# Residual, flushes and norm sums of a Strassen down projection, in a decoder layer on one core

## The chip, the cores and the metric

The kernel runs on one core of a Trainium2 chip. The metric is device time in microseconds of one execution. Before the change three timed runs took 2051.57, 2054.89 and 2056.43 us; the median is 2054.89 us.

## The reference, cut to what matters

One decoder layer for 1024 prompt rows and 32 sample rows that share all weights, in fp32. The two feed-forward blocks hold most of the work:

```python
x = x + 0.5 * _swiglu(_rms(x, g1), w1g, w1u, w1d)   # D = 1024, D_FF = 2816
z = _rms(x, gm) @ w_in                               # attention and short convolution
...
x = x + concat([attn_out, conv_out]) @ w_out
x = x + 0.5 * _swiglu(_rms(x, g2), w2g, w2u, w2d)
x = x + sigmoid(_rms(x, gp) @ w_ple_gate) * (p @ w_ple_proj)

def _swiglu(h, w_gate, w_up, w_down):
    return (jax.nn.silu(h @ w_gate) * (h @ w_up)) @ w_down
```

Each block is a gate-up projection (into 2816 columns) and a down projection (back into 1024), and each is followed by an RMS norm that the next projection needs.

## The kernel before, in words

**Layout.** All activations are kept transposed: `X[m]`, m = 0 to 7, is 128 of the 1024 features by all 1056 rows. The rows are worked in two chunks of 528 (`HC`), each in halves of 264 (`HH`). A matmul is 128x128 weights against 128x264, and each product is made of three matmuls, since weights and activations are split into a high and a low part (lines 799 to 801 in the down projection, 440 to 442 in gate-up).

**Seven products for eight.** Gate-up and down use a Strassen-Winograd scheme: seven block products, numbered 1 to 7, serve a 2x2 block of outputs. `segment` (464) issues them in the order 1, 5, 7 of the quad before, 2, 6, 3 and 4 of the quad before. After each product, `step` evacuates PSUM, casts that product's weights for the quad to come (`follow`; ACT casts in line 360, DVE takes the rest in 361), runs what hangs on the step (`then`), and takes two entries off the list `hops`.

**Pairs.** The 22 blocks of hidden features are joined into 11 pairs. `hop_steps` (485) makes from a pair's two blocks the seven operands of the scheme (sums on POOL, splits on ACT and DVE) and stores them to DRAM (`hop`, SP's queue, lines 512 and 516). The down projection reads them back through POOL's queue (842), 528 KB each, seven a pair; SBUF holds four pairs at a time.

**The down projection** walks the list `FLUSH` of 17 entries (row, first pair, end): output rows `row` and `row + 4` over those pairs, 44 pair-rows in all. For each entry SP loads four weight slabs (766) into six buffers, and POOL makes four sums of them (770 to 773). `put` (803) adds a finished PSUM half into X on DVE (806); `load_x` (844) has put the residual, the layer's input, into X first, eight loads of 528 KB at the start of the stage through SP's queue. The last pair, 10, is made while entries 1 and 2 run, through borrowed places (`FRAG10`), and the load of pair 3 stands behind it.

**The end of the stage.** `last_row` tells after which entry a row is complete. `norm_hook` (986) then squares the rows (ACT 281, added up on POOL 282) and splits them for the next projection (`prep`, ACT 293 and DVE 294). `norm_r` (301) sums over the partitions by matmul, does a chain of small DVE instructions for the inverse root, and spreads the result by matmul (318), as one step. The first weight unit of the next projection (`wget`, 512 KB, cast in 179 and 180) is loaded when that projection asks for it.

**What sets the order.** The code's order is a priority only: the program is built with `schedule_with_timeline_sim=True` (1605), so each engine's queue is laid out from a simulated timeline, and an instruction whose inputs are there in that simulation may come long before its place in the code. On the chip each queue then runs in that fixed order.

## Time and profile before

| | |
|---|---|
| median of 3 runs | 2054.89 us (2051.57 to 2056.43) |
| the profiled execution | 2056.14 us, its span 2054.4 us |
| TensorE busy / mean granted clock | 1961.2 us (95%) / 0.973 |
| DVE, ACT, POOL busy | 1388.2, 750.4, 864.2 us |
| DMA moved | 311 MB |
| down projections, from the first matmul of line 799 to the last of line 801 | 517 to 794 us and 1686 to 1955 us |

The profiled execution takes 1.7 us more than its span, which runs from the first to the last instruction. A granted clock of 1.00 is the 2.4 GHz level and 0.50 the 1.2 GHz level; a figure between is the mean of both over a stretch. "Idle before" is time in which an engine had no work in hand, with what ended it.

### The profile page before, as it was taken

The numbers are of one execution on the slowest core, as the hardware profiler recorded it, in microseconds if no ns is written. First come the engines' busy times: TensorE is split into PE (matmuls) and PEld (weight loads), VectorE is DVE, ScalarE is ACT, GpSimd is POOL, SyncE is SP. The second block draws the span as 40 slices with busy tenths as digits, with TensorE's granted clock in tenths as the row PEclk, the third lists the DMA queues.
The fourth block names the chain that finished last, engine by engine and source line by source line (L and its number), as shares of the span: only waits on it lengthen the run. The fifth ranks groups of instructions, "written<-read, shape, count | busy, mean of one in ns | idle before, by whom it ended". The sixth has DMA issues, their size and how long they took to land.

```text
span 2054.4 us, 38467 instructions
## 1 busy us (share of the span) xinstructions
PE 1961.2 (95%) x14639; PEld 1906.3 (93%) x14639; DVE 1388.2 (68%) x2635; ACT 750.4 (37%) x1590; POOL 864.2 (42%) x880
## 2 busy tenths in 40 slices
PE   7999999999699998999999899999999987999999
PEld 6999999999699997999887799999999987999898
DVE  7748877776666676456585367687777756666864
ACT  5324444444222243314344233344444432222531
POOL 2436665555444444003221124375555464443410
PEclk8999999999899998999999899999999998999999
DMA  7126754445976725101012331465454488775231
GB/s 254 67 79 204 229 168 133 153 157 175 359 236 222 246 93 175 36 20 42 21 34 82 100 110 48 140 221 166 143 166 132 133 280 302 247 233 187 80 136 50
DMA packets 184941, 311.15 MB, mean 151 GB/s; under 512 B 20289, under 2 KB 121033, under 8 KB 184628
## 3 DMA queue, kind: packets, MB, share of 16 engines
q1 hardware_dynamic: 160244, 220.23, 33.0%
q0 software_dynamic: 23648, 87.28, 12.4%
q8 instruction: 116, 1.90, 0.4%
q10 hardware_dynamic: 864, 1.18, 0.2%
q14 instruction: 69, 0.57, 0.1%
HBM read 202.50 MB, written 107.82 MB: 151 GB/s over the span
## 4 chain that ended last, share of the span: by engine, by line
PE 83%; DVE 6%; DMA 6%; issue 2%; ACT 1%; POOL 1%; SPq 0%; DVEq 0%; ACTq 0%; POOLq 0%
PE ps L440 11%; PE ps L441 11%; PE ps L442 11%; PE ps L799 7%; PE ps L801 6%; PE ps L800 6%; PE ps L332 4%; PE ps L334 4%; PE ps L333 4%; PE ps L1352 2%; PE ps L1351 2%; PE ps L1350 2%; PE ps L594 2%; PE ps L593 2%; PE ps L592 2%
## 5 line engine op out<-in xcount | busy, mean ns | idle before, releaser
L440 PE MATMUL ps<-bh_a,wh_a 128*128 128x264 f32 x2128 | 604.7, 286 | 16.6 <-DMA x_a<-in_xT_dram 6.7
L441 PE MATMUL ps<-bh_a,wl_a 128*128 128x264 f32 x2128 | 605.3, 285 | 0.0
L442 PE MATMUL ps<-bl_a,wh_a 128*128 128x264 f32 x2128 | 600.5, 284 | 0.0
L440 PEld LDWEIGHTS ps<-bh_a,wh_a 128*128 128x128 f32 x2128 | 400.3, 189 | 20.6 <-issue 12.7
L441 PEld LDWEIGHTS ps<-bh_a,wl_a 128*128 128x128 f32 x2128 | 401.4, 189 | 0.0
L442 PEld LDWEIGHTS ps<-bl_a,wh_a 128*128 128x128 f32 x2128 | 401.1, 189 | 0.0
L799 PE MATMUL ps<-pair_a,vh_a 128*128 128x264 f32 x1232 | 355.0, 293 | 34.7 <-ACT vh_a L360 17.5
L800 PE MATMUL ps<-pair_a,vl_a 128*128 128x264 f32 x1232 | 353.8, 288 | 0.3 <-DVE vl_a L361 0.2
L801 PE MATMUL ps<-pair_a,vh_a 128*128 128x264 f32 x1232 | 353.2, 289 | 0.0
L806 DVE SCALAR_TENSOR_TENSOR x_a<-ps,x_a 128x264 f32<-128x264 f32 x476 | 198.4, 427 | 133.8 <-PE ps L801 116.2
L799 PEld LDWEIGHTS ps<-pair_a,vh_a 128*128 128x128 f32 x1232 | 235.4, 193 | 41.2 <-ACT vh_a L360 19.4
L800 PEld LDWEIGHTS ps<-pair_a,vl_a 128*128 128x128 f32 x1232 | 237.3, 193 | 0.8 <-DVE vl_a L361 0.8
L801 PEld LDWEIGHTS ps<-pair_a,vh_a 128*128 128x128 f32 x1232 | 236.4, 192 | 0.0
L332 PE MATMUL ps<-xnh_a,whi_a 128*128 128x384 f32 (+1 forms) x528 | 173.3, 329 | 12.5 <-DVE x_a L1442 6.5
L333 PE MATMUL ps<-xnh_a,wlo_a 128*128 128x384 f32 (+1 forms) x528 | 171.8, 326 | 0.4 <-DVE wlo_a L180 0.4
L334 PE MATMUL ps<-xnl_a,whi_a 128*128 128x384 f32 (+1 forms) x528 | 171.8, 326 | 0.0
L361 DVE TENSOR_TENSOR wl_a<-ws_a,wh_a 128x512 fp32r<-128x512 f32 x152 | 132.6, 872 | 36.3 <-ACT wh_a L360 36.2
L385 POOL TENSOR_TENSOR ws_a<-wr_a,wr_a 128x512 f32<-128x512 f32 x38 | 50.9, 1339 | 211.5 <-DMA wr_a<-in_w2gu_dram 87.1
L360 ACT CAST vh_a<-dws_a 128x384 fp32r<-128x384 f32 (+2 forms) x136 | 62.9, 467 | 201.1 <-PE ps L801 180.7
L842 POOL DMA_DIRECT2D pair_a<-hop x154 | 83.7, 545 | 116.6 <-PE ps L801 69.8
L360 ACT CAST wh_a<-ws_a 128x512 fp32r<-128x512 f32 x152 | 94.4, 621 | 101.3 <-PE ps L442 87.5
L361 DVE TENSOR_TENSOR wl_a<-wr_a,wh_a 128x512 fp32r<-128x512 f32 x114 | 108.7, 955 | 12.7 <-ACT wh_a L360 11.6
(258 smaller groups left out, 4092.7 us busy)
## 6 DMA issues: line engine op xcount, KB each, us to landing
pair_a<-hop POOLq DMA_DIRECT2D x154, 528.0 KB, 6.8
hop<-sg_a SPq DMA_DIRECT2D x264, 264.0 KB
wr_a<-in_w1gu_dram SPq DMA_DIRECT2D x88, 256.0 KB
wr_a<-in_w2gu_dram SPq DMA_DIRECT2D x88, 256.0 KB
hop<-sge_a SPq DMA_DIRECT2D x88, 132.0 KB
dr_a<-in_w1d_dram SPq DMA_DIRECT2D x48, 192.0 KB
wraw_a<-in_win_dram SPq DMA_DIRECT2D x18, 512.0 KB
dr_a<-in_w2d_dram SPq DMA_DIRECT2D x48, 192.0 KB
```

The costliest lines, as they stand in the source:

```text
L332: nc.tensor.matmul(ps[:, :W], lhsT=wh, rhs=xh, start=(k == 0), stop=False)
L333: nc.tensor.matmul(ps[:, :W], lhsT=wl, rhs=xh, start=False, stop=False)
L334: nc.tensor.matmul(ps[:, :W], lhsT=wh, rhs=xl, start=False, stop=(k == n - 1))
L360: nc.scalar.copy(out=hi, in_=src)
L361: nc.vector.tensor_tensor(out=lo, in0=src, in1=hi.bitcast(F32), op=ALU.subtract)
L440: nc.tensor.matmul(ps[:, :HH], lhsT=wh[:, ks], rhs=bh, start=(start and k == 0), stop=False, skip_group_check=True)
L441: nc.tensor.matmul(ps[:, :HH], lhsT=wl[:, ks], rhs=bh, start=False, stop=False, skip_group_check=True)
L442: nc.tensor.matmul(ps[:, :HH], lhsT=wh[:, ks], rhs=bl, start=False, stop=last, skip_group_check=True)
L799: nc.tensor.matmul(ps[:, :HH], lhsT=wh[:, ks], rhs=bh, start=(start and i == 0), stop=False, skip_group_check=True)
L800: nc.tensor.matmul(ps[:, :HH], lhsT=wl[:, ks], rhs=bh, start=False, stop=False, skip_group_check=True)
L801: nc.tensor.matmul(ps[:, :HH], lhsT=wh[:, ks], rhs=bl, start=False, stop=(i == n - 1), skip_group_check=True)
L806: nc.vector.scalar_tensor_tensor(out=x, in0=ps[:, :HH], scalar=(0.25, -0.25)[up], in1=x, op0=ALU.mult, op1=ALU.add)
```

## The change

Seven things change, in both down projections. The residual is no longer loaded at the start: the first flush of each row writes its first PSUM part into X by ACT with a scale, and the residual comes later, in eight groups of two 264 KB loads, each added by POOL. The list of flushes is divided differently (still 17 entries and 44 pair-rows; the last entry has two pairs instead of one). The last pair is made at entries 5 and 6 from a copy in DRAM, where gate-up now stores blocks 20 and 21, and the load of pair 3 moves from entry 2 to entry 0. A down step takes one entry off `hops` instead of two. Splits of chunk 0 are all prepared with the row, those of chunk 1 all at the end, at other places. The next projection's first weight unit is loaded and split during the last entry. The norm's sums and its spreading stand apart, each behind a projection.

```diff
 FLUSH = [
-    (0, 0, 1), (1, 0, 2), (2, 0, 3), (3, 0, 3), (0, 1, 4), (1, 2, 5), (2, 3, 6), (3, 3, 6), (0, 4, 7),
-    (1, 5, 8), (2, 6, 9), (3, 6, 9), (0, 7, 10), (1, 8, 11), (2, 9, 11), (3, 9, 11), (0, 10, 11),
+    (0, 0, 1), (1, 0, 2), (2, 0, 2), (3, 0, 3), (0, 1, 4), (1, 2, 5), (2, 2, 5), (3, 3, 6), (0, 4, 7),
+    (1, 5, 8), (2, 5, 8), (3, 6, 9), (0, 7, 9), (1, 8, 11), (2, 8, 11), (3, 9, 11), (0, 9, 11),
 ]
+RES = {4: (2, 0), 7: (1, 0), 8: (2, 1), 9: (3, 0), 10: (0, 0), 11: (1, 1), 12: (3, 1), 13: (0, 1)}
...
-    def norm_r(c, name, s, d=2):
+    def norm_r(c, name, s):
...
-        after(d, stat)
+        return sums, spread
...
+    def hop_last(pr, c, src):
+        cell = {}
+        e0 = at("sgl", LASTAT, HH, F32R)
+        def parts(u, n, hi, t, neg=False):
+            split(hi, t.bitcast(F32R), t, neg)
+            for part, v in enumerate((hi.bitcast(F32), t)):
...
+        new = lambda: wtile("hhi", shape=[P, 2, HH], dt=F32R)
+        return hop_sums(cell, src) + [
+            lambda: parts(1, 2, new(), cell["s"][1]),
+            lambda: parts(0, 1, e0, cell["s"][0][:, 0]),
+            lambda: parts(3, 2, new(), cell["a"]),
+            lambda: parts(5, 2, new(), cell["b"], True),
+        ]
...
-            if self.j < 4:
-                nc.sync.dma_start(out=hd[self.j, :, self.ch * HC:(self.ch + 1) * HC], in_=self.g.rearrange("p i t -> p (i t)"))
+            if self.j < 4 or self.j >= FF - 2:
+                nc.sync.dma_start(out=hd[self.j % 16, :, self.ch * HC:(self.ch + 1) * HC], in_=self.g.rearrange("p i t -> p (i t)"))
...
     class DownQuad(Quad):
+        pops = 1
...
-            nc.vector.scalar_tensor_tensor(out=x, in0=ps[:, :HH], scalar=(0.25, -0.25)[up], in1=x, op0=ALU.mult, op1=ALU.add)
+            f = (0.25, -0.25)[up]
+            if first and self.p0 == 0:
+                nc.scalar.activation(out=x, in_=ps[:, :HH], func=AF.Identity, scale=f)
+            else:
+                nc.vector.scalar_tensor_tensor(out=x, in0=ps[:, :HH], scalar=f, in1=x, op0=ALU.mult, op1=ALU.add)
...
-        def load_x(self, *rows):
-            for m in rows:
-                nc.sync.dma_start(out=X[m], in_=self.src[:, m])
+        def residual(self, m, c):
+            t = wtile("res")
+            s = slice(c * HC, (c + 1) * HC)
+            nc.sync.dma_start(out=t, in_=self.src[:, m, s])
+            return lambda: nc.gpsimd.tensor_tensor(out=X[m][:, s], in0=X[m][:, s], in1=t, op=ALU.add)
...
-                    if i in (1, 2) and c == 0:
-                        hops.extend(hop_steps(10, i - 1, from_ring(10, i - 1), FRAG10))
+                    if i in (5, 6) and c == 0:
+                        hops.extend(hop_last(10, i - 5, from_hd(10, i - 5)))
+                    if c == 0:
+                        res = [self.residual(m, RES[i][1]) for m in (RES[i][0], RES[i][0] + 4)] if i in RES else []
+                    else:
+                        for fn in res:
+                            fn()
                     segment(q, prev)
                     prev = q
-                    if i == 2 and c:
-                        while hops:
-                            hops.pop(0)()
+                    if i == 0 and c:
                         self.load(3, 1, 5, 7, 2, 6, 3, 4)
+                    if i == len(FLUSH) - 1:
+                        if c == 0:
+                            st["end"] = self.end
+                            pump_dma()
+                        else:
+                            split_one()
...
+    nst = [norm_r(c, "nm", 9) for c in range(3)]
     for c in range(3):
         ps = proj(U0, c)
+        nst[c][0]()
...
+        ps1 = proj(U0 + 1, c)
+        nst[c][1]()
         k_evac(c, ps)
```

## Rows read from the trace of the kernel before

**Rows 1.** The page's second part: the span in 40 equal slices of 51.4 us; each digit is a tenth, TensorE's busy share first, the granted TensorE clock second.

```profile
PE   7999999999699998999999899999999987999999
...
PEclk8999999999899998999999899999999998999999
```

**Rows 2.** Busy time of each engine in stretches of the first down projection and around it (start:end of the stretch in us, its length, then for PE, PEld, DVE, ACT, POOL the busy us and in brackets the instructions, then the mean granted TensorE clock, the DMA share, GB/s).

```profile
500.00:520.00 20.00, 18.79 (x154) 18.57 (x153) 9.49 (x21) 5.74 (x14) 12.84 (x24) 1.00 0.99 345
520.00:540.00 20.00, 11.14 (x66) 10.06 (x66) 11.80 (x24) 4.83 (x12) 12.24 (x19) 0.83 1.10 401
540.00:560.00 20.00, 14.52 (x96) 14.01 (x96) 14.09 (x31) 4.67 (x10) 3.39 (x5) 0.83 0.91 319
560.00:580.00 20.00, 18.35 (x128) 18.35 (x129) 14.35 (x24) 4.62 (x9) 11.16 (x13) 0.83 0.79 256
580.00:600.00 20.00, 20.00 (x166) 20.00 (x166) 12.52 (x26) 4.83 (x10) 8.22 (x12) 1.00 0.56 176
720.00:740.00 20.00, 18.06 (x136) 17.88 (x135) 9.99 (x25) 3.81 (x8) 8.61 (x10) 0.91 0.28 92
760.00:780.00 20.00, 15.94 (x117) 14.66 (x116) 19.96 (x43) 12.49 (x30) 12.03 (x13) 0.98 0.23 85
580.00:740.00 160.00, 158.06 (x1282) 157.88 (x1282) 104.64 (x214) 36.19 (x71) 70.61 (x92) 0.99 0.66 215
```

**Rows 3.** The same view, the second down projection.

```profile
1680.00:1700.00 20.00, 11.07 (x70) 10.02 (x69) 4.79 (x13) 3.37 (x11) 8.41 (x15) 0.74 1.12 402
1700.00:1720.00 20.00, 10.17 (x58) 8.54 (x58) 13.16 (x31) 5.08 (x12) 9.65 (x13) 0.78 1.07 393
1720.00:1740.00 20.00, 19.73 (x156) 19.51 (x155) 13.30 (x30) 4.87 (x10) 8.18 (x9) 0.96 0.79 244
1740.00:1760.00 20.00, 19.51 (x158) 19.16 (x157) 13.36 (x28) 4.52 (x9) 8.84 (x12) 1.00 0.51 162
1920.00:1940.00 20.00, 17.56 (x134) 16.38 (x132) 19.96 (x43) 13.05 (x32) 12.15 (x14) 1.00 0.11 34
```

**Rows 4.** TensorE's timeline at the start of the first down projection, the matmuls ahead of which it stood still (start, duration, line, operation, and in square brackets the idle time before it and what ended it).

```profile
525.48 0.56 PE L440 MATMUL ps<-bh_a,wh_a 128*128 128x264 f32 x1 [6.69 <-DMA x_a<-in_xT_dram]
...
538.27 0.36 PE L799 MATMUL ps<-pair_a,vh_a 128*128 128x264 f32 x1 [2.25 <-DVE x_a L806]
...
541.28 0.59 PE L799 MATMUL ps<-pair_a,vh_a 128*128 128x264 f32 x1 [1.69 <-DVE x_a L806]
...
561.65 0.81 PE L799 MATMUL ps<-pair_a,vh_a 128*128 128x264 f32 x2 [5.05 <-ACT vh_a L360]
```

**Rows 5.** The same 80 us (500 to 580): what the DMA engines moved, the issue line of the residual load, then from the timelines the longest stretch of SP's queue (start, length, line, what it issued, how many) and POOL's first work after its longest wait.

```profile
DMA packets 11622, 26.42 MB, mean 330 GB/s; under 512 B 1120, under 2 KB 7008, under 8 KB 11616
...
x_a<-in_xT_dram SPq DMA_DIRECT2D x8, 528.0 KB
...
533.49 12.52 SPq L512 DMA_DIRECT2D hop<-sg_a  x5
...
557.99 1.10 POOL L842 DMA_DIRECT2D pair_a<-hop  x2 [16.52 <-DVE sg_a L361]
```

**Rows 6.** The start of the second down projection: three stops of TensorE, then one line each of the timelines of SP, POOL and ACT (the last is a weight cast that waited for its slab).

```profile
1686.16 0.51 PE L799 MATMUL ps<-pair_a,vh_a 128*128 128x264 f32 x2 [2.56 <-ACT vh_a L360]
...
1694.19 0.56 PE L440 MATMUL ps<-bh_a,wh_a 128*128 128x264 f32 x1 [5.55 <-DMA x_a<-xs_d]
...
1717.25 0.81 PE L799 MATMUL ps<-pair_a,vh_a 128*128 128x264 f32 x2 [7.91 <-ACT vh_a L360]
...
1700.49 10.68 SPq L512 DMA_DIRECT2D hop<-sg_a  x4
...
1715.46 0.71 POOL L770 TENSOR_TENSOR dws_a<-dr_a,dr_a 128x256 f32<-128x256 f32 x1 [7.96 <-DMA dr_a<-in_w2d_dram]
...
1685.81 0.30 ACT L360 CAST vh_a<-dr_a 128x128 fp32r<-128x128 f32 x1 [5.60 <-DMA dr_a<-in_w2d_dram]
```

**Rows 7.** Groups of instructions by line and shape (line, engine, operation, out<-in, count, then total busy us and mean ns of one, then idle time before the group).

```profile
L806 DVE SCALAR_TENSOR_TENSOR x_a<-ps,x_a 128x264 f32<-128x264 f32 x476 | 198.4, 427 | 133.8 <-PE ps L801 116.2
...
L565 ACT COPY g_a<-ps 128x264 f32<-128x264 f32 x76 | 28.1, 370 | 33.6 <-PE ps L442 33.6
...
L675 POOL TENSOR_TENSOR nt<-x_a 128x528 f32<-128x528 f32 x8 | 12.2, 1524 | 18.5 <-DVE bl_a L361 14.4 <-DVE x_a L665 4.1
```

**Rows 8.** TensorE's timeline at the two ends: the matmuls ahead of which it stood still.

```profile
778.57 0.39 PE L799 MATMUL ps<-pair_a,vh_a 128*128 128x264 f32 x1 [2.85 <-DVE x_a L806]
...
785.86 0.39 PE L799 MATMUL ps<-pair_a,vh_a 128*128 128x264 f32 x1 [0.85 <-DVE x_a L806]
...
788.40 0.58 PE L332 MATMUL ps<-xnh_a,whi_a 128*128 128x384 f32 x2 [1.91 <-ACT whi_a L179]
...
814.31 1.62 PE L318 MATMUL ps<-ident,pr 128*128 128x128 f32 x6 [3.33 <-DVE pms L308]
...
1941.77 0.39 PE L799 MATMUL ps<-pair_a,vh_a 128*128 128x264 f32 x1 [2.85 <-DVE x_a L806]
...
1978.04 0.44 PE L332 MATMUL ps<-xnh_a,whi_a 128*128 128x384 f32 x1 [1.97 <-DVE pth L1493]
```

**Rows 9.** Two stretches of 4 us at the first end, columns as in Rows 2.

```profile
780.00:784.00 4.00, 3.87 (x20) 3.40 (x19) 4.00 (x11) 2.20 (x6) 2.05 (x4) 0.65 0.53 178
816.00:820.00 4.00, 3.84 (x17) 3.75 (x18) 2.66 (x14) 0.97 (x2) 0.00 (x0) 0.50 0.40 135
```

More of the change, by code (lines that the diff above doesn't have):

```diff
@@ L457, in step @@
                 fn()
-            for _ in range(2):
+            for _ in range(self.pops):
                 if hops:
@@ L500, in t2, with hop_steps @@
             pool(out=cell["b"][:, 1], in0=cell["a"][:, 1], in1=o[:, 0], op=add)
[L502 to L503 removed]
+        return [t1, t2]
+    def hop_steps(pr, c, src):
+        cell = {}
+        e0 = [at("sge", FRAG[0] + HH * part, HH, F32R) for part in range(2)]
+        two = [[at("sg", FRAG[1 + 2 * i + part], HC, F32R) for part in range(2)] for i in range(3)]
         v2 = lambda t: t.rearrange("p (i t) -> p i t", i=2)
[L506 to L508 removed]
         def store(i):
             for part in range(2):
[L512 removed]
+                nc.sync.dma_start(out=hop_dst(pr, c, 1 + 2 * i, 2, part), in_=v2(two[i][part]).bitcast(F32))
         def store_e():
@@ L827, in out4 @@
         def out4(self):
[L828 removed]
+            self.put(self.b, 1, 0, True)
             now[0] += 1
@@ L1502, in tile_decoder_layer @@
         ple_proj(m)
+    nst = [norm_r(c, "np", 9) for c in range(3)]
     for c in (0, 1):
@@ L1505, in tile_decoder_layer @@
             ple_gate(m, c)
-    for m in (0, 1):
-        ple_gate(m, 2)
-        wdone(UG + m)
-        for c in range(3):
-            ple(m, c)
+            nst[c][m]()
+    ple_gate(0, 2)
+    wdone(UG)
+    nst[2][0]()
+    for c in (0, 1):
+        ple(0, c)
+    ple_gate(1, 2)
+    wdone(UG + 1)
+    nst[2][1]()
+    ple(0, 2)
+    for c in range(3):
+        ple(1, c)
     for m in range(2, 8):
```

101 lines of the change are left out of this document (43 added, 58 removed).

## The prediction

> **What bounds the kernel now.** The slices come first [rows 1]. TensorE is the engine that sets the time: its digit is 9 nearly throughout, and where it falls, the granted clock often falls too. Two dips lie at the starts of the down projections (slices 11 and 34), weaker ones behind their ends. The stretches put a size on them [rows 2, 3]. At full clock TensorE issues 166 matmuls of 264 columns in 20 us (580 to 600), so one is worth 20/166 = 0.1205 us. From 500 to 580 it issued 154 + 66 + 96 + 128 = 444 of 664: 220 are missing, **26.5 us**. From 1680 to 1760 it issued 442, which is **26.7 us**. In 580 to 740 only the dip at 720 to 740 (30 matmuls, 3.6 us) stands out, so mid stage there is nothing to win, only something to spoil. At the ends, 760 to 780 lacks 49 (5.9 us) and 1920 to 1940 lacks 32 (3.9 us), with DVE busy 19.96 of 20 us in both.
>
> Next, what TensorE waited for. At the first start it stands 6.69 us for the residual load, 2.25 and 1.69 us for puts, 5.05 us for a weight cast [rows 4]. The DMA engines are full: 0.99, 1.10, 0.91 in three stretches [rows 2], 26.42 MB in 80 us, of which the residual is 8 x 528 KB = 4.3 MB [rows 5]. The 5.05 us has its own cause: POOL stood 16.52 us behind the load of pair 3, which waited for splits of pair 10, and the next weight sums stood behind that load; meanwhile five hop stores held SP's queue, in which weight slabs also travel, for 12.52 us [rows 5]. At the second start the stops are 2.56, 5.55 and 7.91 us: a slab still under way, the residual, and a slab again, as four hop stores held SP for 10.68 us and POOL then waited 7.96 us [rows 6]. Between stops TensorE ran partly at 1.2 GHz: the granted 0.83 of 560 to 580 means (1 - 0.83) x 20/0.5 = 6.8 us at half speed, 3.4 us of work lost behind the 5.05 us stop [rows 2, 4].
>
> **The starts.** Removed: eight residual loads, both chunks of pair 10's splits and stores, and the wait that they put ahead of pair 3. Moved to ACT: the first PSUM part of 32 halves a stage, 32 x 0.427 = 13.7 us off DVE, at 0.370 us each on ACT by the nearest row, another read of 264 columns out of PSUM [rows 7]. In entry 0 that is 8 x 0.37 = 3.0 us beside seven casts of 256 columns (0.30 us at 128 [rows 6], so some 0.4, an estimate), 5.8 us against 42 x 0.1205 = 5.1 us of matmuls; gate-up's last products fill the same time, so I charge nothing, at worst 1 us a stage. Added ahead of the stage: four stores of 264 KB (blocks 20 and 21), 0.3 us of issue each on SP. Pair 3, loaded after entry 0 instead of 2, is needed only in entry 4, after 1+2+2+3 = 8 pair-rows = 40 us; its seven issues of 0.55 us [rows 5], 3.9 us of POOL, now stand ahead of the weight sums for entry 2, which have entry 1's 10 us to run in. The transfers left until then are about 26.4 - 4.3 - 3.8 (pair 10's stores: 2 chunks x 14 x 132 KB) + 1.1 = 19.4 MB, 48 us at the 401 GB/s of [rows 2], from about 502: done near 550, pair 3 wanted near 560. It fits, narrowly, and weight slabs still travel in the crowd.
>
> What stays? Below, nothing: then all slabs come in time, as they do from 580 on. Above, the slab stops of both starts together: 2.56 + 5.05 + 7.91 plus 3.4 us of slow clock, 19 us. I take 2.56 (a slab late before any of this began) + 3 for a second one + 3.4 = **9 us** a start, nearer the lower end because the two queues' stops named above lose their cause. Gain: 17.5 + 17.7 = 35.2 us.
>
> A page speaks against the change. The trace shows the first slab arriving late enough for a 5.60 us wait of ACT while pair loads fill the engines [rows 6]. The Trainium skill, "DMA: Bandwidth & Descriptors", section "Queues, rings and completion order", says that each DMA engine takes turns between the queues it has work for, a packet at a time. By that rule SP's slabs go on alternating with POOL's pair loads whatever leaves SP's own queue, so late slabs stay for as long as pairs 0 to 3 arrive; the sum would be that of rival A.
>
> **Mid stage.** Sixteen POOL additions of 128x528 a stage: the nearest row gives 1.52 us [rows 7], 24 us, on a POOL busy 70.6 of 160 us [rows 2]; it would stand at 59%. Sixteen loads of 264 KB are the same 4.3 MB, where DMA was at 0.66 of its time. The additions stand in POOL's queue ahead of pair loads, weight sums behind them; each waits for its transfer and for a row whose flush is an entry old. What pays if it blocks is the next entry's casts. Bounds: 0, and one stop of 5.05 us for each of 16 groups (81 us, rival B). POOL has 40% left and slabs run an entry ahead, so I charge 3 us in all. Pair 10's work is the same number of instructions at another time; its four reloads a stage add 1.1 MB, nothing. The dip at 720 to 740 I leave.
>
> **The ends.** First end: 5.9 us to 780, then stops of 0.85, 1.91 and 3.33 us [rows 8], and half clock, by (1 - granted)/0.5 x 4 us x 1/2: 1.4 us in 780 to 784 and 2.0 us in 816 to 820 [rows 9]; together 15.4 us. The DVE-bound part has a plain size. The last two entries make 28 puts, 12.0 us, seven splits and six or more `prep` parts, over 20 us, in 3 x 42 matmuls = 15.2 us. With two pairs in the last entry there are 4 x 42 = 20.2 us for it: the 5.9 and 3.9 us should go down to about 1. The 1.91 us wait for the first weight unit goes: it is loaded and cast an entry earlier. The 3.33 us wait for the root chain is covered by a projection (24 matmuls of 384 columns), unless the DVE backlog, now with all of chunk 1's splits at the end, takes longer; half of it and of the slow clock stay, and with 1 us of the first terms I keep **5 us**. Chunk 2's split places lie under pair 9, which the last entry now reads to its end, so those eight parts come after it; they are hidden behind the four projections of chunks 0 and 1 that run first, and if not, rival C pays for them. Second end: 3.9, the 1.77 us of the 2.85 that fall after 1940, and 1.97 [rows 3, 8] = 7.7; I keep 2.7. Gain 10.4 + 5.0 = 15.4 us.
>
> **Sum.** 35.2 + 15.4 - 3 = 47.6 us. The profiled execution took 2056.14 us, 1.25 above the median shown, so 2008.5 for one like it, **2007** as a median.
>
> **Rivals.** *A, the start stays bound by transfers* (or pair 10 is planned forward again: queues follow a simulated timeline, so its move is a lower priority and no date). For it: DMA at 1.10, and the 2.56 us stop that has nothing to do with residual or hops. Against: 8 MB leave. Then only the residual stops go, 6.69 and 5.55, with about 2 us of clock each: 16.2 instead of 35.2 us, **2026**. Chance 0.20.
>
> *B, POOL is blocked* by residual additions waiting for their transfers, with pair loads and weight sums behind. For it: the 16.52 us wait, which cost TensorE 5.05. If all 16 groups cost 5.05 us in place of the 3 charged: 2007 - 3 + 81 = **2085**; it decides from 50.6/5.05, ten groups, on. Against: mid stage DMA and POOL have room. Chance 0.05 for slower, and 0.04 that it eats just the gain.
>
> *C, the ends stay bound by DVE*: 28 puts and all of chunk 1's and 2's `prep` in one place; for it, 19.96 of 20 us busy. The 15.4 us stay lost: **2022**. Chance 0.13.
>
> **The numbers.** Forecast 0.58, A 0.20, C 0.13, B 0.05 slower and 0.04 no change. The forecast's own range, with 0 to 19 us staying at each start and 0 to all at the ends, is about 1990 to 2022; A and C reach to 2030, and what of A falls together with C is left out, as is all of B: 1989 to 2032. A measurement of this kernel can tell about 0.2%, 4 us, from no change; faster by more has 0.91, within 0.04, slower 0.05.
>
> **What would show it.** Right: no residual wait and no stop over 3 us at the starts, over 600 matmuls of 264 columns in the first 80 us, a clock of 1.00 there in most stretches; DVE below 19 us in 20 at the ends and no wait for the first weight unit; mid stage still 166 in 20 us. Wrong: weight casts waiting for slabs at the start (A), POOL's weight sums behind an addition that waits for a transfer (B), DVE full from the last entry into the next projection (C). A saving below 20 us would make the forecast wrong.

## The result: 20 us won where 47 were forecast

The changed kernel takes 2033.52 us (median of four runs, 2031.0 to 2035.1), the kernel before, on the same chip, 2053.23: a ratio of **0.990, 95% interval 0.988 to 0.992**. The change makes the kernel faster by some 20 us. The forecast was 2007 us, and its range began 1989 and ended 2032, so the result lies 1.5 us outside.

The slices of the profile after, to be held against [rows 1] (tenths of busy time and of the granted clock in 40 equal slices): the dips at slices 11 and 33 to 34 are shallower and still there, and slice 16, behind the first end, is lower than before.

```profile
PE   7999999999899997999999799999999998999999
...
PEclk7999999999899998999999899999999999999999
```

Busy times and clock in the stretches of [rows 2, 3] and a few beside them, in the same columns:

```profile
500.00:520.00 20.00, 20.00 (x167) 20.00 (x166) 9.49 (x23) 6.20 (x15) 10.35 (x19) 1.00 0.87 287
520.00:540.00 20.00, 13.12 (x87) 12.06 (x86) 6.42 (x16) 4.95 (x15) 7.93 (x16) 0.87 1.12 399
540.00:560.00 20.00, 17.13 (x113) 16.44 (x113) 11.12 (x23) 8.61 (x24) 11.46 (x16) 0.79 0.86 304
560.00:580.00 20.00, 18.04 (x133) 17.62 (x132) 10.89 (x20) 10.09 (x24) 14.57 (x15) 0.91 0.67 205
580.00:600.00 20.00, 20.00 (x166) 20.00 (x165) 15.64 (x27) 6.40 (x14) 10.77 (x17) 1.00 1.06 344
700.00:720.00 20.00, 18.66 (x152) 18.41 (x151) 15.54 (x29) 4.49 (x10) 11.50 (x14) 1.00 0.94 319
720.00:740.00 20.00, 20.00 (x164) 19.79 (x163) 17.35 (x35) 6.39 (x13) 10.94 (x10) 1.00 0.13 37
760.00:780.00 20.00, 19.10 (x138) 18.63 (x138) 19.99 (x36) 13.00 (x27) 16.08 (x23) 1.00 0.52 158
800.00:820.00 20.00, 15.24 (x90) 14.57 (x91) 8.77 (x42) 3.64 (x8) 0.00 (x0) 0.72 0.36 112
1680.00:1700.00 20.00, 15.29 (x92) 14.19 (x91) 9.10 (x24) 7.80 (x24) 11.61 (x19) 0.83 1.12 397
1700.00:1720.00 20.00, 16.91 (x127) 15.71 (x127) 11.53 (x21) 10.46 (x27) 9.78 (x11) 1.00 0.77 254
1720.00:1740.00 20.00, 19.29 (x156) 18.88 (x155) 11.88 (x21) 7.90 (x20) 13.28 (x15) 1.00 0.80 244
1740.00:1760.00 20.00, 20.00 (x165) 20.00 (x166) 15.12 (x31) 5.58 (x12) 8.18 (x11) 1.00 1.08 372
1920.00:1940.00 20.00, 19.14 (x125) 18.96 (x124) 19.34 (x33) 12.89 (x25) 10.26 (x9) 1.00 0.84 285
```

With 166 matmuls in 20 us as the full number, 500 to 580 lacks 164 (19.8 us; 26.5 before) and 1680 to 1760 lacks 124 (14.9; 26.7 before). DVE is still full at the ends (19.99 and 19.34 of 20 us), but at the first end TensorE now gets 138 matmuls in 760 to 780 (117 before), and the first down projection's last matmul comes at 780.3 us instead of 793.8. The stretch 1920 to 1940 is not to be held against the one before: the second down projection now ends inside it, at 1933.6 us (1955.3 before). The dip of 720 to 740 is gone; a smaller one stands at 700 to 720.

TensorE's stops in the first stage, which answer to [rows 4, 8] (start, duration, line, operation, the idle time before it and what ended it):

```profile
530.96 0.39 PE L828 MATMUL ps<-pair_a,vh_a 128*128 128x264 f32 x1 [3.45 <-DVE g_a L605]
...
537.02 0.36 PE L828 MATMUL ps<-pair_a,vh_a 128*128 128x264 f32 x1 [2.47 <-DMA pair_a<-hop]
...
542.85 0.84 PE L828 MATMUL ps<-pair_a,vh_a 128*128 128x264 f32 x2 [2.22 <-ACT x_a L837]
...
564.18 0.39 PE L828 MATMUL ps<-pair_a,vh_a 128*128 128x264 f32 x1 [1.96 <-ACT x_a L837]
...
803.43 0.98 PE L324 MATMUL ps<-ident,pr 128*128 128x128 f32 x3 [8.44 <-DVE pms L312]
```

No stop names the residual any more, and neither POOL's 16.52 us wait nor SP's 12.52 us [rows 5] is left. In their place stand a product of gate-up's last block (3.45 us), a pair unit (2.47), two puts on ACT (2.22, 1.96), and at the end the 3.33 us stop ahead of the matmul that spreads the norm has become 8.44 us. Most of those at the start lead back to ACT's and SP's queues. Two casts from ACT's timeline of the same run:

```profile
528.76 0.41 ACT L364 CAST sgl_a<-hd 128x264 fp32r<-128x264 f32 x1 [2.30 <-DMA hd<-hd]
...
541.43 0.41 ACT L364 CAST vh_a<-dws_a 128x256 fp32r<-128x256 f32 x1 [6.45 <-POOL dws_a L799]
```

And two entries of SP's queue there (start, length, line, what was issued, how many), with POOL's product of the last block behind them:

```profile
513.25 0.44 SPq L565 DMA_DIRECT2D hd<-hd  x1
...
531.87 9.20 SPq L607 DMA_DIRECT2D hd<-g_a  x2
...
539.96 0.76 POOL L602 TENSOR_TENSOR g_a<-g_a,u 128x264 f32<-128x264 f32 x1
```

ACT's cast `sgl_a<-hd` is **pair 10's**, of entries 5 and 6 in the code, and it runs at 528.76, nine microseconds into the stage, which begins at 520; its block was read back by SP at 513.25, ahead of the stage. It waited 2.30 us, and the tanh of gate-up's last block stood behind it. The cast at 541.43 waited 6.45 us for a weight sum that POOL made only between its pair loads; two puts stood behind it. SP was held 9.20 us by the store of the last block, whose product POOL made only at 539.96.

**Where the time went**, by the legs between the first and last matmuls of each part in the two profiled executions (22.1 us apart): the down projections became 16.9 and 13.6 us shorter (277.0 to 260.1 and 269.1 to 255.5), the leg behind the first one 5.2 us longer, and the first matmul of L828 came 3.4 us later. That last is not the change: over the profiles of this study that matmul lies anywhere from 516.4 to 523.0 us, and at 516.8 and 522.6 (e7, e4) in two kernels whose queues are the same up to there.

For all that follows, a stage's loss (the time that full-rate matmuls would not have needed) is divided in three: *start* is from 20 us ahead of the first matmul of the down projection to 60 us behind it, *mid* the next 160 us, *end* from there to its last matmul, each the length of the stretch less 0.1205 us for every matmul in it.

| kernel | ratio to before (95%) | start 1 / 2 | mid 1 / 2 | end 1 / 2 |
|---|---|---|---|---|
| before | 1 | 26.4 / 27.5 | 5.4 / 1.9 | 14.3 / 11.0 |
| after | 0.990 (0.988 to 0.992) | 20.7 / 16.4 | 4.1 / 4.8 | 3.5 / 3.4 |
| e9 flushes and ends only | 0.993 (0.991 to 0.995) | 21.8 / 25.8 | 2.0 / 2.4 | 3.6 / 3.5 |
| e10 e9 + pair 10 moved | 0.999 (0.998 to 1.001) | 29.8 / 30.8 | 3.7 / 2.4 | 3.9 / 3.6 |
| e13 e9 + residual later | 0.990 (0.988 to 0.992) | 17.6 / 21.4 | 4.7 / 4.1 | 3.2 / 3.5 |
| e7 after, old flushes | 0.999 (0.998 to 1.000) | 23.6 / 18.7 | 7.3 / 8.2 | 12.4 / 10.9 |
| e1 after, pair 10 held back | 0.991 (0.990 to 0.993) | 15.4 / 12.6 | 10.6 / 9.1 | 3.5 / 3.4 |
| e2 after, sums on DVE | 0.988 (0.987 to 0.990) | 16.6 / 16.4 | 5.2 / 5.8 | 3.6 / 3.5 |
| e5 after, pairs in order | 0.991 (0.989 to 0.993) | 20.6 / 19.4 | 6.1 / 5.5 | 3.5 / 3.5 |
| e8 e1 + e2 + e4 + e5 | **0.982 (0.980 to 0.984)** | 14.4 / 7.3 | 7.0 / 6.1 | 3.2 / 3.3 |
| e16 after, 3.7 MB fewer | 0.984 (0.982 to 0.987) | 10.2 / 12.3 | 9.4 / 5.3 | 3.0 / 3.4 |

### The profile page after: what moved, and what is told of

The parts are those of the page before. It is cut to its first block, busy times and chain, and to the rows that moved or that the text cites. A ratio compares the mean times of both kernels' runs of the same rounds, so it can differ in the third digit from the quotient of the medians.

```text
span 2032.3 us, 38555 instructions
## 1 busy us (share of the span) xinstructions
PE 1955.5 (96%) x14639; PEld 1904.3 (94%) x14639; DVE 1375.5 (68%) x2571; ACT 769.4 (38%) x1654; POOL 912.6 (45%) x912
## 3 DMA queue, kind: packets, MB, share of 16 engines
q0 software_dynamic: 23648, 87.28, 12.6%
## 4 chain that ended last, share of the span: by engine, by line
PE 82%; DMA 6%; DVE 6%; issue 2%; POOL 2%; ACT 1%; SPq 0%; DVEq 0%; POOLq 0%; ACTq 0%
PE ps L446 11%; PE ps L447 11%; PE ps L448 11%; PE ps L828 7%; PE ps L830 7%; PE ps L829 7%; PE ps L336 4%; PE ps L338 4%; PE ps L337 4%; PE ps L1388 2%; PE ps L1389 2%; PE ps L1387 2%; PE ps L620 2%; PE ps L619 2%; PE ps L621 2%
## 5 line engine op out<-in xcount | busy, mean ns | idle before, releaser
L828 PE MATMUL ps<-pair_a,vh_a 128*128 128x264 f32 x1232 | 355.9, 292 | 25.2 <-ACT x_a L837 8.8
L828 PEld LDWEIGHTS ps<-pair_a,vh_a 128*128 128x128 f32 x1232 | 234.6, 191 | 31.7 <-ACT x_a L837 10.3
L839 DVE SCALAR_TENSOR_TENSOR x_a<-ps,x_a 128x264 f32<-128x264 f32 x412 | 171.3, 425 | 90.4 <-PE ps L830 79.1
L365 DVE TENSOR_TENSOR wl_a<-ws_a,wh_a 128x512 fp32r<-128x512 f32 x152 | 131.8, 867 | 35.7 <-ACT wh_a L364 35.2
L336 PEld LDWEIGHTS ps<-xnh_a,whi_a 128*128 128x128 f32 x528 | 102.0, 193 | 15.9 <-DVE x_a L1479 8.6
```

The lines of the kernel that those rows point to most:

```text
L336: nc.tensor.matmul(ps[:, :W], lhsT=wh, rhs=xh, start=(k == 0), stop=False)
L365: nc.vector.tensor_tensor(out=lo, in0=src, in1=hi.bitcast(F32), op=ALU.subtract)
L828: nc.tensor.matmul(ps[:, :HH], lhsT=wh[:, ks], rhs=bh, start=(start and i == 0), stop=False, skip_group_check=True)
L839: nc.vector.scalar_tensor_tensor(out=x, in0=ps[:, :HH], scalar=f, in1=x, op0=ALU.mult, op1=ALU.add)
```

## The experiments

### Which part of the change made the 20 us

**e9: only the flushes and the ends.** In the changed kernel the residual and pair 10 are put back, with two entries of `hops` taken a step and pair 3's load at entry 2 as before:

```diff
-RES = {4: (2, 0), 7: (1, 0), 8: (2, 1), ...}
+RES = {}
-            if first and self.p0 == 0:
+            if False:
...
+                    5: [lambda: self.load_x(0, 4)], 3: [lambda: self.load_x(1, 5), ...
-                    if i in (5, 6) and c == 0:
-                        hops.extend(hop_last(10, i - 5, from_hd(10, i - 5)))
+                    if i in (1, 2) and c == 0:
+                        hops.extend(hop_steps(10, i - 1, from_ring(10, i - 1), FRAG10))
```

> Of the change only the other division of the flushes and the parts at the ends are made (splits of chunk 1 at the end, first weight unit in the last entry, norm sums and spreading apart); the residual is loaded at the start and added with the first PSUM part by DVE as before, pair 10 is made at entries 1 and 2 and pair 3 loaded at entry 2 as before. Theory 5 (the division of the flushes is worth most of the gain: 10.8 and 7.6 us in the last 50 us of the two down projections, less the new stop behind the root chain): 2038 to 2043 us, ratio 0.992 to 0.995. Rival (the gain came from the starts, as the prediction had it, and the ends bring the 3 + 5 us read between 740 and 840 and 1900 and 1980): 2045 to 2050 us, ratio 0.996 to 0.9985.

Measured: 2038.5 us, 0.993, theory 5's. The division of the flushes with the ends is worth 15 us of the 20, though the profile still has the residual's stops of 6.69 and 5.67 us and the 5.04 and 8.59 us of weight casts.

**e10: the same with pair 10 moved.** 

> The run before this one with pair 10 made at entries 5 and 6 and pair 3 loaded at entry 0 as in the changed kernel: against the changed kernel only the residual is undone (loaded at the start, eight loads of 528 KB; first PSUM part added to it by DVE). Theory 6 (the start is bound by the amount of transfers, and the 4.3 MB of the residual are what the change took out of it; 6.69 and 5.55 us of stops before): the starts lose 10 to 16 us of what they gained, 2042 to 2050 us, ratio 0.995 to 0.999. Rival (the residual's loads only filled the same wait; POOL's sums and pair 10 bound the start): within 4 us of the changed kernel, ratio 0.989 to 0.992; then the time between this run and the one before it is pair 10's.

Measured: 2052.9 us, 0.999: **pair 10's move costs 13 us** while the residual is at the start. Pair 3's load moved with it, from entry 2 to entry 0, and no run with the residual at the start parts the two. One long stop in each start is behind it, on TensorE's timeline, where e9 has 5.04 and 8.59 us:

```profile
557.64 0.81 PE L828 MATMUL ps<-pair_a,vh_a 128*128 128x264 f32 x2 [16.16 <-ACT vh_a L364]
...
1722.01 0.81 PE L828 MATMUL ps<-pair_a,vh_a 128*128 128x264 f32 x2 [15.77 <-ACT vh_a L364]
```

ACT's waits at the first (who waited for whom: total us, times, longest):

```profile
ACT vh_a L364 <- DMA dr_a<-in_w1d_dram: 13.8, 1, 13.8
```

ACT waited that long for a weight slab to land, and 16.4 us for one at the second start, while pair loads, the residual and pair 10's reads and stores shared the engines. The residual's later place then wins 19 us (0.999 to 0.990), more than the theory's 10 to 16.

**e13: pair 10 put back alone** (the last four lines of the diff above, with two entries a step and pair 3's load behind pair 10 as in e9). 

> The changed kernel with pair 10 made at entries 1 and 2 through the old places, two steps of it at a time, and the load of pair 3 behind it at entry 2, as before; the residual stays later, the flushes and ends stay changed. Theory 8 (planned forward, pair 10 of the changed kernel costs the start what it cost without the residual's move, 13 us, or a good part of it): 2021 to 2028 us, ratio 0.984 to 0.987. Rival (the prediction's view: once the residual has left, pair 10's stores, its splits and the wait ahead of pair 3 are what holds POOL and SP, and their move gains): the 5 us wait for a weight cast near 560 and the 8 us one near 1711 are back, 2037 to 2045 us, ratio 0.992 to 0.996.

Measured: 2034.2 us, 0.990: neither theory. With the residual out of the way, pair 10's move is worth nothing that can be told (its interval with the changed kernel's allows some 5 us either way). And with pair 10 in its old place the residual's move wins 6 us (0.993 to 0.990), not 19. As the rival said, the weight cast's 5.1 us stop near 556 is back; the second start has 6.48 us for a put instead.

**e7: the old list of flushes in the changed kernel.** Only `FLUSH` is the list of before. 

> The list of flushes of the kernel before in the changed kernel: one pair in the last entry instead of two; nothing else is undone. Theory 5 (the ends were bound by DVE, and the second pair in the last entry gives DVE the time for its puts and splits; the end gained less than forecast only because of the 8.44 us stop behind the unit loads): windows around both ends lose 20 to 50 matmuls, DVE is busy 19.9 of 20 us again, the time rises by 4 to 10 us, ratio 0.992 to 0.995. Rival (the flushes' division does nothing at the ends; what was gained there came from the early unit load and from the norm's two parts): within 2 us, ratio 0.989 to 0.991.

Measured: 2053.0 us, 0.999. Without the new list **nothing measurable is left of the 20 us**, twice what the theory wanted. In the profile the two down projections are 25.3 us longer and the other legs, the 3.4 us of the opening among them, 8.7 shorter. 8.9 and 7.5 us are at the ends, where DVE is full for longer (stretches as above):

```profile
760.00:780.00 20.00, 17.12 (x122) 15.16 (x120) 20.00 (x46) 14.10 (x36) 15.46 (x19) 1.00 0.37 119
780.00:800.00 20.00, 16.39 (x84) 15.38 (x84) 16.81 (x19) 7.22 (x15) 14.60 (x22) 0.91 0.64 206
1920.00:1940.00 20.00, 18.23 (x132) 16.28 (x130) 19.99 (x49) 14.40 (x36) 13.20 (x14) 1.00 0.25 76
1940.00:1960.00 20.00, 17.22 (x93) 16.88 (x94) 19.11 (x32) 9.61 (x18) 9.79 (x9) 0.91 0.60 223
```

By the table some 6 us a stage are lost besides, at the starts, which take in the 20 us ahead of the stage, and mid stage. The old list's entry 2 needs pair 2 as well, the new one's only pairs 0 and 1; that this is the reason was not tested.

### What still holds the starts

**e1: pair 10 really at entries 5 and 6.** A one-column copy out of X ahead of its loads makes them wait for entry 4's and 5's first parts:

```diff
     def from_hd(pr, c, behind=None):
-        t = [tmp3("hd0"), tmp3("hd1")]
+        t = [...]; [nc.vector.tensor_copy(out=t[i][:, 0, 0:1], in_=X[behind][:, 0:1]) for i in range(2) ...]
```

> Each load of pair 10's two blocks gets a one-column DVE copy out of X ahead of it, from the row of entry 4 (chunk 0) or entry 5 (chunk 1), so that pair 10 cannot be made before that entry's first PSUM parts are in X; nothing else is changed. Theory 1 (the starts fell short because pair 10's casts, splits and stores were planned forward into them): the stops of 3.45 us at 531 and 2.75 us at 1687, each behind an ACT cast of pair 10 that waits for its load, go, the windows 500 to 580 and 1680 to 1760 gain 15 to 60 matmuls each, and the time falls by 4 to 10 us against the changed kernel, to 2024 to 2030 us, ratio to the kernel before 0.986 to 0.989. Rival (the starts are bound by the transfers of pairs 0 to 3 and by POOL that issues them): the next late slab or sum takes the place of these stops, the time stays within 3 us of 2033.5, ratio 0.989 to 0.992.

Measured: 2035.2 us, 0.991, the rival's number, though the theory's mechanism is in the profile: both stops behind pair 10's casts are gone. Two others on TensorE's timeline:

```profile
536.26 0.56 PE L828 MATMUL ps<-pair_a,vh_a 128*128 128x264 f32 x1 [6.47 <-DMA pair_a<-hop]
...
617.80 0.39 PE L828 MATMUL ps<-pair_a,vh_a 128*128 128x264 f32 x1 [2.51 <-DVE x_a L839]
```

A pair unit is now waited for 6.47 us at the same place (2.47 and 0.96 before), and what the starts gained, 5.3 and 3.8 us, comes back mid stage, 6.5 and 4.3 us: DVE stands behind POOL's sums of pair 10 there, and once 4.04 us ahead of the copy that this edit added, so part of that loss is the edit's own.

**e2: sums on DVE.** `DownWeights` takes `add = nc.vector.tensor_tensor` for entries 0 to 3, and line 602 uses DVE for block 21. 

> The weight sums of entries 0 to 3 and the last block's second product of gate and up are made on DVE instead of POOL; nothing else is changed. Theory 2 (POOL's queue, held by pair loads that wait for earlier pair loads to land, brings the weight sums and the last product late, and ACT's casts, the puts behind them and SP's store of 9.2 us wait for those): the stops of 2.2 and 2.0 us behind ACT's puts and SP's 9.2 us go, the first start gains 20 to 50 matmuls, the time falls by 4 to 8 us to 2025 to 2030 us, ratio 0.986 to 0.989. Rival (the slabs themselves come late, since the engines are full of pair loads): the casts wait for DVE sums that wait for slabs, and DVE has 16 more additions of up to 0.5 us in each start: no change or 1 to 4 us longer, 2033 to 2038 us, ratio 0.990 to 0.993.

Measured: 2029.3 us, 0.988, the theory's end, 4 us below the changed kernel; the two intervals overlap, so the 4 us are not clear of noise. SP's 9.20 us is gone (a store at 532.04 takes 0.32), and the loss falls in the first start only.

**e3: the first put on DVE** instead of ACT (`tensor_scalar` with the factor). 

> The first PSUM part of each half is written into X by DVE with a scale (0.43 us) instead of ACT; nothing else is changed. Theory 2a (a put on ACT costs TensorE because it stands in ACT's queue behind casts that wait for weight sums): the stops at the starts that name ACT x_a, 3.45 - not counted - then 2.22, 1.96 and 2.75 us, go or halve, the time falls by 2 to 5 us, ratio 0.987 to 0.989. Rival (ACT's puts save DVE time that the starts need, as the prediction had it, 13.7 us a stage): DVE becomes what the first entries wait for, 2 to 8 us longer, ratio 0.991 to 0.994.

Measured: 2037.3 us, 0.992 (0.990 to 0.994). The theory falls, and the time is the rival's: ACT's puts save some 4 us if anything, since this interval too overlaps the changed kernel's. A put takes 0.39 us on ACT in the changed profile; 0.37 was estimated.

**e5: pairs 2 and 3 behind pairs 0 and 1.** The built program of the changed kernel loads units in this order (pair.unit), the last units of entry 0's own pair, 0.3 and 0.4, behind ten others, six of them of pairs 2 and 3:

```
0.1 0.5 0.7 1.1 0.2 0.6 1.5 1.7 2.1 2.5 3.2 1.2 1.6 2.2 2.6 3.6 0.3 0.4 1.3 1.4 ...
```

```diff
+    behind = lambda pr, o: (pr == 3 or pr == 2 and o in (1, 5, 2, 6)) and nc.vector.tensor_copy(
+        out=unit(pr, o)[:, 0:1], in_=X[0][:, (pr - 2) * HC:(pr - 2) * HC + 1])
...
-                nc.gpsimd.dma_start(out=unit(pr, o), ...
+                behind(pr, o); nc.gpsimd.dma_start(out=unit(pr, o), ...
```

> In the changed kernel POOL's queue loads the seven units of pairs 0 and 1 that entry 0 and 1 need last (3 and 4) only after four units of pair 2 and two of pair 3, 3.2 MB that no entry needs for 25 us or more. Here a one-column copy out of X, from the first PSUM part of entry 0, stands ahead of those loads of pair 2 (chunk 0's part) and of all of pair 3 (chunk 1's part), so that they come behind all of pairs 0 and 1; nothing else is changed. Theory 4 (the starts are bound by transfers, and the order in which the pairs come decides which wait TensorE sees: 6.47 us for a pair unit in the run without pair 10, 2.47 + 0.96 in the changed kernel): the waits for pair units in the first start go, pair 10's stops of 3.45 and 2.75 us stay, the first start gains 15 to 40 matmuls, the time falls by 2 to 5 us, ratio 0.9875 to 0.989. Rival (the amount decides, not the order: DMA at 1.12 of its time for 20 us whatever comes first): pairs 2 and 3 come late in their turn, or slabs do, and the time stays within 2 us or rises, ratio 0.989 to 0.992.

Measured: 2035.2 us, 0.991: the rival. No pair unit is waited for any more; weight casts are, 3.25 and 2.42 us, and puts. **e6** has this order and e1's copies. 

> The order of the pair loads of the run before this one together with pair 10 held back to entries 5 and 6. Theory 4 together with theory 1 (each of the two hides behind the other: with pair 10 away the wait for the pair unit rose from 2.47 + 0.96 to 6.47 us): both stops go, the windows 520 to 560 hold 40 or more matmuls more than the 200 of the changed kernel, and the time falls by 6 to 10 us, more than the two changes one by one, ratio 0.985 to 0.987. Rival (the amount of the transfers decides): a third wait takes the place, within 3 us of the changed kernel, ratio 0.9885 to 0.992.

Measured: 2036.1 us, 0.992, again the rival: casts 4.60 us, a put 2.73, and mid stage 11.3 and 9.4 us lost. So one wait taken away only shows the next.

**e8: e1, e2, e5 and e4 (below) together.** 

> All four edits together: pairs 2 and 3 behind pairs 0 and 1, pair 10 held back to entries 5 and 6, the weight sums of entries 0 to 3 and block 21's product on DVE, unit splits 2 to 5 behind the first root chain. If the causes are those of theories 1 to 4 and each has its own time: 3.2 (chain) + 4.2 (sums on DVE) as measured + 6 to 10 for order and pair 10: 2016 to 2021 us, ratio 0.982 to 0.985. Rival (the start is bound by the amount of transfers, and the DVE's 16 sums fill the room that is won): only chain and half of the sums, 2026 to 2030 us, ratio 0.986 to 0.989.

Measured: **2016.9 us, 0.982**, the first theory's, and the fastest of the kernels that leave nothing out, 17 us below the changed kernel, where e1, e2, e5 and e4 by themselves bring 0, 4, 0 and 3, none of them clear of noise. Its stretches:

```profile
520.00:540.00 20.00, 15.06 (x105) 14.57 (x104) 9.76 (x36) 6.25 (x19) 7.27 (x15) 0.83 1.11 388
540.00:560.00 20.00, 18.23 (x147) 17.80 (x146) 10.06 (x28) 9.55 (x25) 1.74 (x5) 1.00 0.83 297
560.00:580.00 20.00, 17.57 (x131) 17.36 (x130) 11.42 (x22) 7.31 (x17) 10.60 (x13) 0.91 0.56 175
1680.00:1700.00 20.00, 18.23 (x147) 17.80 (x146) 10.23 (x27) 9.19 (x24) 3.16 (x6) 1.00 1.08 387
1700.00:1720.00 20.00, 17.57 (x131) 17.36 (x130) 11.72 (x22) 7.31 (x17) 9.79 (x12) 0.91 0.57 177
1720.00:1740.00 20.00, 18.69 (x154) 18.48 (x153) 12.29 (x28) 6.21 (x13) 10.50 (x16) 1.00 1.01 329
```

The second start loses 7.3 us, DMA is as full as ever (1.11, 1.08) and POOL much emptier (1.74 us in 540 to 560 and 3.16 in 1680 to 1700, where the changed kernel has 11.46 and 11.61). The longest stop left in the first start, 4.94 us at 532.17, is for a product of gate-up's last block.

Two runs leave one edit out, a third replaces one; none leaves out e2 or e4. **e11, without e1:** 

> The four edits together without the one that holds pair 10 back (so it is planned forward into the start again). Theory 7 (pair 10 in the start costs ACT and DVE there what it costs later, 5 us, and only the order of the pairs and the sums on POOL bind): within 3 us of 2017, ratio 0.980 to 0.983. Rival (with order and sums mended, pair 10's casts are the next bound of the start): 2022 to 2028 us, ratio 0.984 to 0.987.

Measured: 2046.0 us, 0.996, with runs from 2038 to 2053. Further than the rival: pair 10, planned forward, costs over 20 us once the rest is mended. These three edits without e1 are even some 11 us slower than none of them (0.996 against 0.990), so their worth hangs on pair 10's place. **e12, without e5:** 

> The four edits together without the order of the pair loads (four units of pair 2 and two of pair 3 ahead of the last of pairs 0 and 1 again). Theory 4b (with the sums off POOL, the order of the transfers is what TensorE waits for): the wait of some 6 us for a pair unit is back in the first start, 2022 to 2028 us, ratio 0.984 to 0.987. Rival (the order is hidden; sums and pair 10 did it): within 3 us of 2017, ratio 0.980 to 0.983.

Measured: 2024.0 us, 0.986. The rival's size of the effect is excluded, the order is worth 7 us here; but the wait for a pair unit is not back, the loss is mid stage (11.1 and 12.4 us), so the theory has the number and not the place. **e14, with pair 10 made at entries 1 and 2** as in e13 instead of e1: 

> The run before this one with the sums of entries 0 to 3 and block 21's product on DVE, pairs 2 and 3 behind pairs 0 and 1, and the unit splits behind the root chain: the combination that took 2017 us, with pair 10 made early instead of at entries 5 and 6. Theory 8b (made early through its own places, pair 10 is as cheap as made late): 2014 to 2021 us, ratio 0.981 to 0.984. Rival (pair 10 has to leave the start): 2024 to 2035 us, ratio 0.985 to 0.991.

Measured: 2022.3 us, 0.984 (0.983 to 0.986), between the two.

**e16, e17: fewer transfers.** The products of pair 2 read pair 3's units, pair 2 is not loaded, and pair 6 is held back. This leaves out work that the result needs, and with the seven loads also POOL's seven issues, 3.8 us a start:

```diff
-                u = unit(self.p0 + i, o)
+                u = unit(3 if self.p0 + i == 2 else self.p0 + i, o)
-            for o in ops:
+            for o in ops if pr != 2 else ():
+                pr == 6 and nc.vector.tensor_copy(out=unit(pr, o)[:, 0:1], in_=X[2][:, 0:1]); ...
```

> The changed kernel without the loads of pair 2: products of pair 2 read pair 3's units instead (so the sums are of the wrong pair; matmuls, weights and everything else are as many as before), and pair 6, which comes into pair 2's place, is held back to entry 6. That takes 7 loads of 528 KB, 3.7 MB or 9.2 us at 400 GB/s, and 3.8 us of issue on POOL out of each start. Theory A (the starts are bound by the amount of the transfers): each start loses 6 to 9 us less, 2016 to 2022 us, ratio 0.982 to 0.985. Rival (late sums, pair 10's casts and the order of queues bind it; the transfers only look full): within 3 us a start, 2028 to 2034 us, ratio 0.9875 to 0.9905.

Measured: 2023.3 us, 0.984, in theory A's ratio, though neither start is in its 6 to 9 us. The starts lose 10.5 and 4.1 us less, and 5 us of the first come back mid stage. The first start's stretches:

```profile
520.00:540.00 20.00, 17.37 (x127) 16.67 (x126) 10.20 (x26) 8.45 (x26) 9.67 (x15) 0.91 1.11 395
540.00:560.00 20.00, 17.33 (x132) 16.16 (x131) 14.16 (x25) 10.15 (x27) 11.74 (x14) 1.00 0.66 207
560.00:580.00 20.00, 19.50 (x160) 19.28 (x160) 13.45 (x22) 8.21 (x20) 13.22 (x16) 1.00 0.88 278
```

> The same in the combination that took 2017 us (sums of entries 0 to 3 and block 21's product on DVE, pairs 2 and 3 behind pairs 0 and 1, pair 10 held back, unit splits behind the root chain). Theory A: the 14 and 7 us that its starts still lose fall to 5 or less each, 2005 to 2009 us, ratio 0.976 to 0.978. Rival (what is left there is weight preparation on ACT and DVE): within 3 us of 2017, ratio 0.980 to 0.983.

Measured: 2010.6 us, 0.979: 6 us below e8, just outside theory A's number. So these seven loads a stage, with their issues, are worth 10 us in the changed kernel and 6 where queues and order are mended. Taken alone in the changed kernel that is the largest hold found; in the mended kernel pair 10's place (e11) is a larger one.

### The end of the first stage

**e4: unit splits behind the root chain.** In the changed kernel DVE's timeline has the chain behind three splits of weight units whose loads SP issued late:

```profile
794.27 2.48 DVE L183 TENSOR_TENSOR wlo_a<-wraw_a,whi_a 128x1024 fp32r<-128x1024 f32 x2 [7.17 <-ACT whi_a L182]
796.66 0.15 DVE L316 TENSOR_SCALAR pms<-ps 128x3 f32<-128x3 f32 x1
800.22 1.22 DVE L183 TENSOR_TENSOR wlo_a<-wraw_a,whi_a 128x1024 fp32r<-128x1024 f32 x1 [3.40 <-ACT whi_a L182]
801.36 0.16 DVE L255 TENSOR_SCALAR pr<-pms 128x3 int32<-128x3 int32 x1
```

The sums were ready at 796.66, the chain began at 801.36. SP issued the loads late because three stores of X stood ahead of them in its queue:

```profile
766.76 17.45 SPq L1040 DMA_DIRECT2D xm_d<-x_a  x3
789.46 7.64 SPq L172 DMA_DIRECT2D wraw_a<-in_win_dram  x4
```

The edit puts a one-column copy of the chain's result into the units' places:

```diff
-        hi = at("whi", unit_at(i), 1024, F32R)
+        hi = at(...); 2 <= i < 6 and nc.vector.tensor_copy(out=hi[:, 0:1], in_=root["nm", 0][:, 0:1])
```

> At the end of the first down projection the casts of weight units 2 to 5 of the next projection are put behind the first root chain (a one-column copy out of its result goes into each unit's place ahead of the cast); nothing else is changed. Theory 3 (the root chain stands in DVE's queue behind splits of units whose loads come late, and the spreading matmul, and TensorE with it, wait 8.44 us for that): the stop at the spreading falls below 2 us, the time falls by 5 to 8 us to 2026 to 2029 us, ratio 0.986 to 0.988. Rival (the late unit loads bound that stretch themselves: TensorE waits for units 2 or 3 a little later instead): the stop moves to the first matmul of a later unit, the time stays within 2 us of 2033.5, ratio 0.989 to 0.991.

Measured: 2030.4 us, 0.989 (0.987 to 0.990). The stop is 2.31 us, and the leg behind the first down projection 90.3 us instead of 95.0 (89.8 before the change): the 5.2 us lost there were this queue. The whole time falls by 3 us, less than forecast and not clear of noise; in the profile the opening and the second down projection are 2.4 and 1.9 us longer, which nothing here explains. TensorE's stop:

```profile
799.01 1.41 PE L324 MATMUL ps<-ident,pr 128*128 128x128 f32 x5 [2.31 <-DVE pms L312]
```

**e15: e4 with sums and spreading in one place.** 

> The changed kernel with the unit splits behind the root chain, as in the run that took 2030 us, but the norm's sums and its spreading in one place, behind the first projection, in the first end; nothing else is changed. Theory 9 (a projection between them covers the chain): each of three chains is waited for again, 2 to 3 us for the first and less for the others, 3 to 6 us in all, 2033 to 2037 us, ratio 0.990 to 0.992. Rival (the plan put a projection between them anyway, or other waits hide it): within 2 us of 2030, ratio 0.9875 to 0.9895.

Measured: 2027.6 us, 0.988, the rival's: in the first end, setting the two apart is worth nothing that these runs show.

## Why the prediction was wrong

**The starts: 35.2 us forecast, 16.8 measured** (5.7 and 11.1). The step that failed is "I take 2.56 + 3 + 3.4 = 9 us a start, nearer the lower end because the two queues' stops named above lose their cause". 20.7 and 16.4 us stayed, about the upper bound that the text had worked out, 19. Both parts of the 9 were too small. TensorE's idle time in the 80 us of each start, by its busy column, fell from 17.2 and 19.5 to 11.7 and 8.5 us, where 5.6 of stops had been kept. What it lost while counted as busy, 9.3 and 7.2 before, is 8.1 and 6.4, where 3.4 had been kept; the granted clock is 0.87, 0.79 and 0.91 in 520 to 580 and 0.83 in 1680 to 1700.

The causes named did go; two others that the text had held for rivals took their place. First the transfers (rival A): DMA stands at 1.12 in 520 to 540 (1.10 before), and taking 3.7 MB out with their issues (e16) wins 15 us at the starts. The step "done near 550" was nearly right, and did not help. The end of the crowd in the changed kernel, columns as in [rows 2], and what moved in 500 to 580:

```profile
540.00:554.00 14.00, 11.78 (x73) 11.51 (x73) 6.63 (x13) 5.67 (x16) 7.28 (x10) 0.70 1.11 396
554.00:560.00 6.00, 5.35 (x42) 4.93 (x41) 4.49 (x10) 2.94 (x9) 4.17 (x6) 1.00 0.28 90
...
DMA packets 11258, 23.90 MB, mean 299 GB/s; under 512 B 1151, under 2 KB 6387, under 8 KB 11251
```

The engines were full until 554, some 4 us later than forecast, and 19.3 MB had moved by then; 23.9 MB moved in all, where 19.4 were forecast, since some of pair 10's transfers were still in the stretch. But "It fits, narrowly" asked only when all is there; TensorE asks for its own unit and slab, and those stand behind loads that nobody needs yet. Second, pair 10 was indeed planned forward, as the bracket in rival A has it. By e13 its move is worth nothing, and it costs 13 us in e10 (with pair 3's load) and over 20 in e11. A pair load took 12.1 us from issue to landing in 498 to 545 and 5.9 us in 600 to 700 (medians), and in e10 one slab in each start kept ACT 13.8 and 16.4 us. The Trainium skill's rule of turns between the queues ("DMA: Bandwidth & Descriptors", "Queues, rings and completion order") spoke for this side; that slabs come late while pair loads fill the engines agrees with it, but no run here tells turns from the plain length of a queue.

Rival A gave 16.2 us for the starts, and 16.8 came; the close number is luck. It counted only the residual's stops. By the table 6.3 of the 16.8 came with the flushes and ends (e9), 8.6 with the residual's later place (e13 against e9) and 1.9 with pair 10's move. As a mechanism it had a chance of 0.20, and a forecast that rests on "done near 550, wanted near 560" should have given it more.

**The ends: 10.4 + 5.0 forecast, 13.6 measured**, in other pieces, so the near sum is partly luck (by its own rows the 7.7 that it set for the second end is 7.64). DVE's part was too small: 10.8 and 7.6 us went from the last entries of the two stages, against 5.9 + 3.9 read from two stretches; the loss lay spread over the last 50 us. Given back was 5.2 us behind the first end (0.4 more was won behind the second). "The 3.33 us wait for the root chain is covered by a projection" failed: it became 8.44 us, by a queue's order and not by DVE's backlog (e4). Rival C's own mechanism, DVE full, is there (19.99 of 20 us) and cost little, since the last entry now has the matmuls to go with it.

**What was not seen: the list of flushes works beyond the ends.** The text spoke of the list at the ends alone. With the old list back (e7), nothing measurable of the 20 us is left, and by the table some 6 us a stage of the loss lie away from the ends.

**Mid stage: 3 us charged, 1.6 measured** (7.3 to 8.9 lost); right in size, with two effects in it: the flushes and ends win 2.9 us there (e9), the residual costs 4.4 (e13 against e9). Rival B did not come: the 32 residual additions took 1.43 us each and POOL waited 10.2 us ahead of them, and no stop over 2 us follows. **Moved puts: charged nothing;** e3 puts them at a gain of some 4 us at most, not clear of noise.

These parts add up to 28.8 us. By the legs, which leave out the 20 us ahead of each stage, it is 25.7, and the 3.4 us by which the first down projection began later make it the 22 us between the two profiles.

## What to carry to other kernels

Where several things hold a stretch at once (transfers, a queue, work planned forward), taking out one shows the next: four edits worth 0, 4, 0 and 3 us alone were worth 17 together, and three of them without e1 cost some 11. So price a removed wait by what is late next, and take the upper bound when the engines that feed the stretch stay full. Where queues are laid out by a simulated timeline, a step moved in the text need not have moved on the chip: pair 10 stayed in the start until a dependency held it back (e1), and the built order of the queue shows that before any run.
